# Weighing unit 1 of a mixture of softmaxes in pairs of heads

**Chip, cores, metric.** One core of one Trainium2 chip; the time is the device time of one launch in microseconds (us).

## The reference, cut to what matters

```python
batch, seq, vocab, num_heads = 32, 128, 4096, 4
prior_probs = softmax(prior)              # over the 4 heads
p = softmax(logits)                       # over the vocabulary, per head
mixture = sum over heads of prior_probs[..., None] * p
```

The 4096 rows (batch x seq) are worked in 32 units of 128 rows, counted from 0. A unit reads 4 heads x 128 rows x 16 KB = 8.39 MB and writes 2.10 MB, all float32.

## The kernel before

ScalarE takes the exponential of each head and sums it on the way; a reciprocal on VectorE and a small product on GpSimd make the four weights; VectorE adds up the four weighted heads ("terms", lines 175 and 181). `m` is how many heads are weighed at once: 4 in most units, 2 in the last four. The code is shortened; the waits for an output buffer to be stored are left out.

```python
es = (lt[:, 0], ebuf1, ebuf2, ebuf3)            # where head 0..3's exponentials go
def exp(h): ...      # ScalarE; for h > 0 it waits until unit u-1's term h has been read
def weigh(h, n): ... # n reciprocals on VectorE, n products on GpSimd; waits for exp h+n-1
def add(h): ...      # VectorE; add(0) overwrites the sum, add(1..3) add to it

m = H if u < U - 4 else 2
for h in range(H):
    if h == 2 and 0 < u < U - 3:
        store(u - 1, obuf[:, (u - 1) % 2], nc.scalar)   # issued by ScalarE, in its order
    exp(h, ...)
    if (h + 1) % m:
        continue
    g = h + 1 - m
    mul = weigh(g, m, ...)
    for k in range(g, h + 1):
        add(k, mul)
if u + 2 < U:
    load(u + 2)     # into the tile that unit u has read; waits for unit u's first term
```

There are two input tiles and two output buffers. All loads go through SyncE's queue, 28 of the 32 stores through ScalarE's.

The softmax here doesn't subtract the row's maximum and nothing guards it: scores larger than these inputs give would overflow.

Of the kernel before, what the change touches and what calls it, by code (L numbers as in the profile page):

```python
# [36 lines left out]
def kernel(  # L37
# [8 lines left out]
    B, S, H, V = logits.shape  # L46
# [6 lines left out]
    U = G * J  # L53
# [13 lines left out]
    def only(ins, *keep):  # L67
        for k in keep:
            tc.add_manual_dep(
                ins.ins,  # L70
                k.ins.name,
                mybir.DependencyInfo(mybir.DependencyClass.Sync, mybir.DependencyReason.DATA),
                reason="all that this instruction waits for",
            )
        tc.declare_no_dep(
            ins.ins,
            group="loop",
            keep=[k.ins for k in keep] + before.get(ins.ins.engine, []),
            reason="covered by the waits that are kept",
        )  # L80
        tc.add_to_no_dep_group("loop", ins.ins)
        before[ins.ins.engine] = [ins.ins]
        return ins
# [4 lines left out]
    exps = {}  # L88
    adds = {}
    stores = {}  # L90

    def load(u):
        if u == 0 or u >= U - 3:
            cuts = (0, 2, 3, 4) if u == U - 1 else (0, 2, 4)
        else:
            cuts = (0, H)
        for h, to in zip(cuts, cuts[1:]):
            ld = nc.sync.dma_start(  # L98
                out=ltile[:, u % 2, h:to], in_=lg[u // J, u % J, :, h:to, :]
            )  # L100


            if u >= 2:
                only(ld, adds[u - 2, 0] if h == 0 else exps[u - 2, to - 1])
            else:
                only(ld)
            for k in range(h, to):
                loads[u, k] = ld

    def store(u, acc, eng, lo=0, hi=V):  # L110
        st = eng.dma_start(out=ov[u // J, u % J, :, lo:hi], in_=acc[:, lo:hi])  # L111
        stores[u] = only(st, adds[u, H - 1])
# [18 lines left out]

    with tc.manual_schedule():
        load(0)
        nc.scalar.dma_start(out=pr, in_=pv)
        load(1)
        nc.gpsimd.memset(pn, 0.0)  # L136
        nc.vector.reduce_max(pmax, pr, axis=AX.X)  # L137
        nc.vector.tensor_sub(pr, pr, pmax.unsqueeze(2).to_broadcast([G, R, H]))  # L138
        nc.scalar.activation(pr, pr, AF.Exp)  # L139
        nc.vector.reduce_sum(pmax, pr, axis=AX.X)  # L140
        nc.vector.reciprocal(pmax, pmax)  # L141
        nc.vector.tensor_mul(  # L142
            pn[0:G].rearrange("g h r -> g r h"), pr, pmax.unsqueeze(2).to_broadcast([G, R, H])
        )
        pq = pn.rearrange("g h (p j) -> g j h p", j=J)
        for t in range(P // 32):
            nc.vector.transpose(pp[32 * t : 32 * (t + 1)], pq[:, :, :, 32 * t : 32 * (t + 1)])  # L147

        for u in range(U):
            bufd = u < U - 2  # L150
            lt = ltile[:, u % 2]
            acc = obuf[:, u % 2] if bufd else lt[:, 0]
            es = (lt[:, 0], ebuf1, ebuf2, ebuf3) if bufd else [lt[:, h] for h in range(H)]
            ppu = pp[:, u % J, :, u // J]

            def exp(h, *keep):
                ex = nc.scalar.activation(  # L157
                    es[h], lt[:, h], AF.Exp, accum_out=dsum[:, u, h : h + 1]
                )
                keep = (loads[u, h],) + keep  # L160
                if bufd and h and u:
                    keep += (adds[u - 1, h],)
                exps[u, h] = only(ex, *keep)

            def weigh(h, n, *keep):
                rc = nc.vector.reciprocal(rden[:, u, h : h + n], dsum[:, u, h : h + n])  # L166
                only(rc, exps[u, h + n - 1])
                mul = nc.gpsimd.tensor_mul(  # L168
                    coeff[:, u, h : h + n], rden[:, u, h : h + n], ppu[:, h : h + n]
                )  # L170
                return only(mul, rc, *keep)

            def add(h, mul, lo=0, hi=V):
                if h == 0:
                    st = nc.vector.tensor_scalar(  # L175
                        out=acc[:, lo:hi], in0=es[h][:, lo:hi], scalar1=coeff[:, u, h : h + 1],
                        scalar2=None, op0=ALU.mult,
                    )
                    adds[u, h] = only(st, mul)
                else:  # L180
                    st = nc.vector.scalar_tensor_tensor(  # L181
                        out=acc[:, lo:hi], in0=es[h][:, lo:hi], scalar=coeff[:, u, h : h + 1],
                        in1=acc[:, lo:hi], op0=ALU.mult, op1=ALU.add,
                    )
                    adds[u, h] = only(st, mul, adds[u, h - 1])



            free = (stores[u - 2],) if bufd and u >= 2 else ()

            m = H if u < U - 4 else 2
            for h in range(H):
                if h == 2 and 0 < u < U - 3:
                    store(u - 1, obuf[:, (u - 1) % 2], nc.scalar)
                exp(h, *(free if m == H and h == H - 1 else ()))
# [3 lines that stand above are left out]
                mul = weigh(g, m, *(free if m < H and g == 0 else ()))  # L199
                for k in range(g, h + 1):  # L200
                    n = 2 if u == U - 1 and k == H - 1 else 1
                    w = V // n
                    for c in range(n):
                        add(k, mul, c * w, (c + 1) * w)
                        if n > 1:
                            store(u, acc, nc.sync, c * w, (c + 1) * w)
            if u + 2 < U:
                load(u + 2)
            if u == U - 3:
                store(u - 1, obuf[:, (u - 1) % 2], nc.sync)  # L210
                store(u, acc, nc.sync)
            elif u == U - 2:
                store(u, acc, nc.sync)
# [30 lines left out]
```

## Time and profile before

| | before |
|---|---|
| median of 3 runs | 780.93 us (780.85 to 780.97) |
| busy: VectorE, ScalarE, GpSimd | 67%, 60%, 1% of the span |
| bytes moved | 335.65 MB, 431 GB/s over the span |
| one unit in the steady part | 24.17 us |

No compute engine is near its limit, and the bytes alone take most of the time. The prediction below shows the lines and reads them. In all lines of a profile DVE is VectorE, ACT is ScalarE, POOL is GpSimd and SP is SyncE; a q behind the name means the engine's sequencer, which issues transfers.

### The profile page before, as it was taken

What the parts mean: (1) busy time and instruction counts of PE and PEld (TensorE: products, weight loads), DVE (VectorE), ACT (ScalarE), POOL (GpSimd) and SP (SyncE); (2) the same over time, 40 slices, a digit from 0 to 9 for tenths busy, and PEclk for the clock granted to TensorE, in tenths of its full rate; (3) what the DMA queues carried; (4) which work ended last, traced back from release to release, by engine and by line L of the source; (5) the groups of instructions that cost most, each with busy time, mean ns of one, the idle gap of its engine ahead of it and who ended that gap; (6) DMA issues with size and microseconds to landing.
All of it is one profiled execution on the core that took longest, in us unless ns stands there. A gap on an engine that the chain in (4) does not pass through costs nothing.

```text
span 779.3 us, 628 instructions
## 1 busy us (share of the span) xinstructions
DVE 521.0 (67%) x174; ACT 470.0 (60%) x258; POOL 8.3 (1%) x41
## 2 busy tenths in 40 slices
DVE  4447865568655686556875558755587555788986
ACT  4476555765557655577555675556755567557782
POOL 0000000000000000000000000000000000000000
DMA  9999999999999999999999999999999999999998
GB/s 407 457 417 397 474 407 417 444 455 434 404 468 401 460 420 416 458 443 418 417 468 407 454 407 468 420 415 447 415 459 417 459 402 464 410 427 431 434 429 379
DMA packets 10117, 335.65 MB, mean 431 GB/s; under 512 B 1137, under 2 KB 1137, under 8 KB 1153
## 3 DMA queue, kind: packets, MB, share of 16 engines
q1 hardware_dynamic: 6048, 276.83, 82.3%
q10 hardware_dynamic: 4064, 58.79, 17.6%
q14 instruction: 5, 0.03, 0.0%
HBM read 268.50 MB, written 67.11 MB: 431 GB/s over the span
## 4 chain that ended last, share of the span: by engine, by line
DVE 55%; ACT 26%; DMA 15%; issue 2%; ACTq 1%; POOL 1%; DVEq 0%; SPq 0%; POOLq 0%
DVE obuf L181 45%; ACT ebuf L157 24%; DMA ltile<-in_logits_dram 9%; DVE obuf L175 8%; DMA out_dram<-obuf 6%; ACT ltile L157 1%; ACTq L111 1%; DVE ltile L181 1%; POOL coeff L168 1%; DVE rden L166 1%; DVEq L239 0%; SPq L98 0%; POOLq L239 0%; POOLq L168 0%
## 5 line engine op out<-in xcount | busy, mean ns | idle before, releaser
L181 DVE SCALAR_TENSOR_TENSOR obuf<-ebuf,coeff,obuf 128x4096 f32<-128x4096 f32 x90 | 403.6, 4484 | 3.8 <-POOL coeff L168 0.6
L157 ACT ACTIVATE ebuf<-ltile 128x4096 f32<-128x4096 f32 x90 | 323.7, 3597 | 39.6 <-DVE obuf L181 32.2
L157 ACT ACTIVATE ltile<-ltile 128x4096 f32<-128x4096 f32 x38 | 137.3, 3614 | 247.6 <-DMA ltile<-in_logits_dram 247.6
L166 DVE RECIPROCAL rden<-dsum 128x4 f32<-128x4 f32 (+1 forms) x36 | 6.3, 175 | 230.3 <-ACT ebuf L157 227.5
L175 DVE TENSOR_SCALAR obuf<-ltile,coeff 128x4096 f32<-128x4096 f32 x30 | 70.6, 2353 | 10.3 <-POOL coeff L168 10.3
L181 DVE SCALAR_TENSOR_TENSOR ltile<-ltile,coeff 128x4096 f32<-128x4096 f32 (+1 forms) x7 | 27.0, 3874 | 0.8 <-POOL coeff L168 0.6
L157 ACT ACTIVATION_READ_ACCUMULATOR ebuf<-ltile 128x1 f32 x90 | 16.8, 186 | 0.0
L168 POOL TENSOR_TENSOR coeff<-rden,pp 128x4 f32<-128x4 f32 (+1 forms) x36 | 7.2, 200 | 755.3 <-DVE rden L166 745.2
L157 ACT ACTIVATION_READ_ACCUMULATOR ltile<-ltile 128x1 f32 x38 | 7.1, 186 | 0.0
L175 DVE TENSOR_SCALAR ltile<-ltile,coeff 128x4096 f32<-128x4096 f32 x2 | 4.7, 2353 | 0.6 <-POOL coeff L168 0.6
L137 DVE TENSOR_REDUCE pmax<-pr 16x256 f32<-16x1024 f32 x1 | 1.2, 1206 | 5.4 <-DMA pr<-in_prior_dram 5.4
L139 ACT ACTIVATE pr<-pr 16x1024 f32<-16x1024 f32 x1 | 1.1, 1055 | 5.7 <-DVE pr L138 5.7
L142 DVE TENSOR_TENSOR pn<-pr,pmax 16x1024 f32<-16x1024 f32 x1 | 1.9, 1925 | 0.1
L140 DVE TENSOR_REDUCE pmax<-pr 16x256 f32<-16x1024 f32 x1 | 1.2, 1208 | 1.1 <-ACT pr L139 1.1
L139 ACT ACT_TABLE_LOAD x1 | 1.3, 1283 | 0.9 <-PEq L228 0.9
L147 DVE STREAM_TRANSPOSE pp<-pn 32x256 f32<-32x256 f32 x4 | 1.7, 436 | 0.1
L141 DVE RECIPROCAL pmax<-pmax 16x256 f32<-16x256 f32 x1 | 1.7, 1741 | 0.0
L138 DVE TENSOR_TENSOR pr<-pr,pmax 16x1024 f32<-16x1024 f32 x1 | 1.2, 1211 | 0.0
L136 POOL MEMSET pn<- 32x1024 f32 x1 | 0.9, 941 | 0.5 <-POOLq L228 0.5
L228 POOL MEMSET const-bfloat16-1.0<- 128x1 bf16 x1 | 0.1, 107 | 0.0
L228 POOL MEMSET const-uint8-127<- 128x1 uint8 x1 | 0.1, 107 | 0.0
L228 POOL MEMSET const-float32-0.0<- 128x1 f32 x1 | 0.1, 103 | 0.2 <-issue 0.2
(1 smaller groups left out, 0.1 us busy)
## 6 DMA issues: line engine op xcount, KB each, us to landing
out_dram<-obuf ACTq DMA_DIRECT2D x28, 2048.0 KB, 28.1
ltile<-in_logits_dram SPq DMA_DIRECT2D x7, 4096.0 KB, 25.5
ltile<-in_logits_dram SPq DMA_DIRECT2D x2, 2048.0 KB, 30.9
out_dram<-obuf SPq DMA_DIRECT2D x2, 2048.0 KB, 33.9
out_dram<-ltile SPq DMA_DIRECT2D x1, 2048.0 KB, 17.2
out_dram<-ltile SPq DMA_DIRECT2D x2, 1024.0 KB, 4.8
ltile<-in_logits_dram SPq DMA_DIRECT2D x28, 29.6
pr<-in_prior_dram ACTq DMA_DIRECT2D x1, 64.0 KB, 5.2
```

Source lines behind the costliest of these rows:

```text
L111: st = eng.dma_start(out=ov[u // J, u % J, :, lo:hi], in_=acc[:, lo:hi])
L137: nc.vector.reduce_max(pmax, pr, axis=AX.X)
L138: nc.vector.tensor_sub(pr, pr, pmax.unsqueeze(2).to_broadcast([G, R, H]))
L139: nc.scalar.activation(pr, pr, AF.Exp)
L141: nc.vector.reciprocal(pmax, pmax)
L142: nc.vector.tensor_mul(pn[0:G].rearrange("g h r -> g r h"), pr, pmax.unsqueeze(2).to_broadcast([G, R, H]))
L147: nc.vector.transpose(pp[32 * t : 32 * (t + 1)], pq[:, :, :, 32 * t : 32 * (t + 1)])
L157: ex = nc.scalar.activation(es[h], lt[:, h], AF.Exp, accum_out=dsum[:, u, h : h + 1])
L166: rc = nc.vector.reciprocal(rden[:, u, h : h + n], dsum[:, u, h : h + n])
L168: mul = nc.gpsimd.tensor_mul(coeff[:, u, h : h + n], rden[:, u, h : h + n], ppu[:, h : h + n])
L175: st = nc.vector.tensor_scalar(out=acc[:, lo:hi], in0=es[h][:, lo:hi], scalar1=coeff[:, u, h : h + 1], scalar2=None, op0=ALU.mult,)
L181: st = nc.vector.scalar_tensor_tensor(out=acc[:, lo:hi], in0=es[h][:, lo:hi], scalar=coeff[:, u, h : h + 1], in1=acc[:, lo:hi], op0=ALU.mu ...
```

## The change

Unit 1's sum should start after two exponentials and not after four. Its first term then ends before exponential 3 has read the tile, so load 3 must now name that exponential as well.

```diff
-                only(ld, adds[u - 2, 0] if h == 0 else exps[u - 2, to - 1])
+                free = [adds[u - 2, 0]] if h == 0 else []
+                if h or u == 3:
+                    free.append(exps[u - 2, to - 1])
+                only(ld, *free)
...
-            m = H if u < U - 4 else 2
+            m = 2 if u == 1 or u >= U - 4 else H
```

## The prediction

> **What bounds the kernel now.** I read the page first (busy shares, the DMA rows, the queues), then the stretches of the span, then the start of the timeline around units 0 to 2, then the queue's own waits and the end of the chain of waits. From the page:
>
> ```profile
> span 779.3 us, 628 instructions
> DVE 521.0 (67%) x174; ACT 470.0 (60%) x258; POOL 8.3 (1%) x41
> DMA  9999999999999999999999999999999999999998
> q1 hardware_dynamic: 6048, 276.83, 82.3%
> q10 hardware_dynamic: 4064, 58.79, 17.6%
> HBM read 268.50 MB, written 67.11 MB: 431 GB/s over the span
> ```
>
> No compute engine is busy more than 67% of the span. The DMA row is at its top digit in all 40 slices but the last, and the two queues add up to 82.3 + 17.6 = 99.9% of what 16 engines can be busy in the span. So the DMA engines have practically no idle time to give back. The stretches of the span (busy time by engine, then clock, DMA share, GB/s) say the same without the averaging:
>
> ```profile
> 1.30:41.70 40.40, 20.59 (x14) 16.59 (x10) 0.77 (x2) 1.00 1.00 431
> 112.50:693.50 581.00, 384.07 (x121) 351.05 (x193) 4.82 (x24) 1.00 1.00 433
> 693.50:749.30 55.80, 49.19 (x19) 43.74 (x25) 1.17 (x6) 1.00 1.00 432
> ```
>
> The reader is to see the last two columns: share 1.00 in the ramp, in the steady part and in the run-up to the end, always at 431 to 433 GB/s, although the compute engines' load differs a good deal. Each unit moves (268.50 + 67.11) / 32 = 10.49 MB, and 10.49 MB at 433 GB/s is 24.2 us. All 335.6 MB at 433 GB/s are 775 us; start-up before the first bytes and the last wait make the rest of the span.
>
> Now the place that the change touches. Unit 0's first exponential starts at 12.67 us, unit 1's at 41.73, unit 2's at 64.72. From the timeline (start, duration, engine and operation, and in brackets the idle time before it and what ended it):
>
> ```profile
> 41.73 3.62 ACT L157 ACTIVATE ltile<-ltile 128x4096 f32<-128x4096 f32 x1 [12.04 <-DMA ltile<-in_logits_dram]
> 45.35 3.60 ACT L157 ACTIVATE ebuf<-ltile 128x4096 f32<-128x4096 f32 x1
> 56.05 0.18 ACT L157 ACTIVATION_READ_ACCUMULATOR ebuf<-ltile 128x1 f32 x1
> 56.27 0.18 DVE L166 RECIPROCAL rden<-dsum 128x4 f32<-128x4 f32 x1 [10.13 <-ACT ebuf L157]
> 56.76 2.35 DVE L175 TENSOR_SCALAR obuf<-ltile,coeff 128x4096 f32<-128x4096 f32 x1 [0.32 <-POOL coeff L168]
> 59.15 13.52 DVE L181 SCALAR_TENSOR_TENSOR obuf<-ebuf,coeff,obuf 128x4096 f32<-128x4096 f32 x3
> 64.72 3.62 ACT L157 ACTIVATE ltile<-ltile 128x4096 f32<-128x4096 f32 x1 [8.48 <-DMA ltile<-in_logits_dram]
> 71.84 0.19 ACT L157 ACTIVATION_READ_ACCUMULATOR ebuf<-ltile 128x1 f32 x1
> 72.70 0.34 ACTq L111 DMA_DIRECT2D out_dram<-obuf  x1
> 73.09 3.59 ACT L157 ACTIVATE ebuf<-ltile 128x4096 f32<-128x4096 f32 x1 [1.06 <-DVE obuf L181]
> 88.32 3.62 ACT L157 ACTIVATE ltile<-ltile 128x4096 f32<-128x4096 f32 x1 [7.92 <-DMA ltile<-in_logits_dram]
> ```
>
> VectorE idles 10.13 us before unit 1's reciprocal: that is the wait that the change attacks. But ScalarE waits for a load before every unit (12.04, 8.48, 7.92 us), and those are the waits that the bytes set.
>
> **What the Trainium skill says.** "DMA: Bandwidth & Descriptors", section "Where 436 GB/s comes from", puts the ceiling of a core's 16 engines at 435.2 GB/s; this trace holds 433 over 581 us, so it agrees and nothing is left above. The same page, "Issuing engines are not separate DMA queues", says that transfers started by different engines run on the same 16 DMA engines and interleave. The trace fits: the stores issued by ScalarE take their 17.6% out of the same 99.9%, and a 2 MB store needs a median 28.1 us to land. So a transfer that is started earlier takes its share from another one in flight. "Perfetto Trace Analysis", section "Optimization Strategy", says to look for gaps on the engine that is the bottleneck and to make what blocks it start sooner. Here that is the DMA, and it has no gap where the change acts.
>
> **The change part by part.**
>
> Removed: unit 1's first term no longer needs exponentials 2 and 3. Exponential 1 with its read-out ends at about 49.04 (45.35 + 3.60, and 0.09 by the read-out). Before, the last read-out ended at 56.23 and the first term began at 56.76, 0.53 later; the same 0.53 gives 49.57 now. VectorE is free by then (unit 0's last term ends at 46.14). First term 49.57 to 51.94, second term (4.49 + 0.03) to 56.46.
>
> Added: one reciprocal (0.18) and one GpSimd product (0.20). The second pair's reciprocal sits behind the second term in VectorE's order; by 56.46 all exponentials are done (56.23), so it costs the same hop less the first wait, about 0.49: third term from 56.95, fourth from 61.47, done at 65.96. Before it was done at 72.67. Unit 1's sum is thus ready 6.7 us sooner, after paying 0.5 us of new hops inside what was idle time.
>
> Moved: two transfers.
> - Load 3 overwrites unit 1's tile. Before it followed the first term (59.13). Now it must follow the first term (51.94) and, by the added condition, exponential 3 (56.23), so it is issued near 56.3: 2.9 us earlier. It stands in the same queue behind load 2, which lands at 64.7 in either case. The 5.6 us that load 3 waits behind it become 8.4 us. Worth on the path: 0.
> - Store 1 is issued by ScalarE in order, after unit 2's second exponential, which ends at 72.03 because load 2 landed at 64.7. So of the 6.7 us only 72.70 - 72.05 = 0.65 us survive. Unit 2's third exponential follows: 72.4 in place of 73.09.
>
> From there on the chain of waits shows a closed loop: two exponentials 7.32, reciprocal and product 0.5, terms 2.36 + 3 x 4.50, store issue 0.34, gaps; 24.17 us from 72.70 to 96.86 and in nearly every unit after. It would carry the 0.65 us forward as earlier stores. The loads, though, follow the bytes. In the steady part ScalarE reaches unit u's third exponential 1.1 to 1.9 us before VectorE lets it go on; this slack shrinks by up to 0.65 us and stays positive or becomes a wait for a load. The sum on the end: removed bytes 0, added DMA gaps 0, so 0 us.
>
> **The end of the kernel.** This decides whether earlier stores can be cashed in:
>
> ```profile
> 701.57 18.07 DMA out_dram<-obuf
> 722.38 26.87 DMA ltile<-in_logits_dram
> 749.28 7.32 ACT ltile L157 x4
> 764.35 4.50 DVE ltile L181
> 768.87 2.35 DVE ltile L181
> ```
>
> The final stretch hangs on a load that lands at 749.28. Before that load the engines have moved all earlier loads and all 28 ScalarE stores (the last one landed about 719.7), and they never paused. So its landing is the sum of those bytes over the rate, whatever the order within. From 749.28 to the last half store (4.8 us to land) nothing of unit 1 takes part. If stores become 0.65 us earlier, load 29 may land that much later, and loads 30 and 31 land when they did.
>
> **The rivals.**
>
> (a) The compute loop is the true bound. For it: its period is the same 24.17 us as the DMA's to the second decimal, and the chain of waits follows it from 72.7 to 701.6 with hardly a gap. Then the 0.65 us reach the end: 780.3. Against it: 8 us of load wait in each unit, and engines without idle time. I give this part of a chance, since two equal periods cannot be told apart in one trace.
>
> (b) The earlier load 3 and store 1 collide. A 2 MB store is 4.8 us of all engines at 433 GB/s; started 0.65 us sooner it takes at most about that from load 3, which lands at up to 88.9 in place of 88.3. Unit 3's slack before its third exponential was 1.6 us, so it is absorbed; if it were not, 781.5.
>
> (c) Head or tail noise: an instruction more on VectorE and GpSimd, another phase of the two queues when the last loads come. The three runs of before span 0.12 us; I allow some tenths, 780.6 to 781.3.
>
> (d) The gain goes through whole: 6.7 us less, 774.2. It would need idle DMA time of that length, which is not there.
>
> **Range and chances.** The central step gives 780.93 + 0 = 780.9. Rival (a) pulls to 780.3, (b) to 781.5, so 8 in 10 lie in 780.3 to 781.4. A change of 2% is 15.6 us, more than twice the whole 6.7 us set free, and slower by 2% would need a DMA gap that nothing here opens: 0.005, 0.99, 0.005.
>
> **What would show it.** Right: unit 1's first term at about 49.6, its last one ending near 66.0; load 3 issued near 56.3, but unit 2 still starting at 64.7 and unit 3 at 88.3 to 88.9; store 1 at about 72.05; DMA share 1.00 at 431 to 433 GB/s as before; the last load landing at 749.3 within a few tenths. It is wrong if unit 2 or 3 starts over 1 us earlier, if the landing at 749.3 moves by over 0.5 us, or if a stretch shows a DMA share well below 1.

## The result, and the profile after

| | runs | median | range |
|---|---|---|---|
| before | 6 | 780.93 us | 780.84 to 781.11 |
| after | 6 | 781.20 us | 781.16 to 781.49 |

The ratio is 1.0004, with a 95% interval of 0.9991 to 1.0017: the same time. (A ratio is the mean time of one kernel's fast runs over that of the other's fast runs of the same rounds, so not quite the ratio of the medians.) The 0.27 us between the medians lie within that interval.

The span is the same (779.3 us in both profiles), yet the chain of waits is a different one. From the page of the kernel before, and below it from that of the changed kernel (shares of the span by engine):

```profile
DVE 55%; ACT 26%; DMA 15%; issue 2%; ACTq 1%; POOL 1%; DVEq 0%; SPq 0%; POOLq 0%
```

```profile
DMA 64%; ACT 27%; DVE 6%; issue 1%; POOL 0%; DVEq 0%; POOLq 0%; ACTq 0%
```

VectorE's terms were 55% of what the end hung on and are 6% now; loads have taken their place. The waits say it in microseconds. Of the kernel before, then of the changed one (who waited for whom, total us, times, longest):

```profile
ACT ltile L157 <- DMA ltile<-in_logits_dram: 247.6, 32, 12.0
...
ACT ebuf L157 <- DVE obuf L181: 32.2, 26, 1.9
```

```profile
ACT ltile L160 <- DMA ltile<-in_logits_dram: 282.2, 32, 12.1
```

ScalarE's 32.2 us of waiting for VectorE are gone (no such line is left), and its waiting for loads has grown by 34.6 us. The change removed a wait in 26 units by touching one, and longer waits for loads took its place.

Here is where it happens. From the timeline of the changed kernel (start, duration, engine and operation; idle time before it):

```profile
49.64 2.35 DVE L178 TENSOR_SCALAR obuf<-ltile,coeff 128x4096 f32<-128x4096 f32 x1 [0.31 <-POOL coeff L171]
...
56.90 9.01 DVE L184 SCALAR_TENSOR_TENSOR obuf<-ebuf,coeff,obuf 128x4096 f32<-128x4096 f32 x2 [0.31 <-POOL coeff L171]
64.31 3.62 ACT L160 ACTIVATE ltile<-ltile 128x4096 f32<-128x4096 f32 x1 [7.98 <-DMA ltile<-in_logits_dram]
65.93 0.34 ACTq L114 DMA_DIRECT2D out_dram<-obuf  x1
...
71.52 3.56 ACT L160 ACTIVATE ebuf<-ltile 128x4096 f32<-128x4096 f32 x1
...
88.50 3.62 ACT L160 ACTIVATE ltile<-ltile 128x4096 f32<-128x4096 f32 x1 [9.69 <-DMA ltile<-in_logits_dram]
...
95.29 0.34 ACTq L114 DMA_DIRECT2D out_dram<-obuf  x1
```

Unit 1's first term starts at 49.64 (before: 56.76) and its last one ends at 65.91. Store 1 goes out at 65.93, 6.77 us sooner than before. Unit 2's third exponential follows its second at 71.52 without a gap (before: 73.09). Store 2 is 1.57 us sooner (95.29 against 96.86). But unit 3 starts at 88.50 against 88.32: its load came no sooner. So the gain is 6.77 us at store 1, 1.57 at store 2 and 0 at load 3. The later stores keep a part of it (ScalarE's last one goes out at 700.71 against 701.57), but the loads do not: the last one lands at 749.09 against 749.28.

### The profile page after: what moved, and what is told of

Same layout as the page of the kernel before. It is cut to its first block, busy times and chain, and to the rows that moved or that the text cites. A ratio compares the mean times of both kernels' runs of the same rounds, so it can differ in the third digit from the quotient of the medians.

```text
span 779.3 us, 631 instructions
## 1 busy us (share of the span) xinstructions
DVE 521.1 (67%) x175; ACT 467.7 (60%) x258; POOL 8.5 (1%) x42
## 3 DMA queue, kind: packets, MB, share of 16 engines
q1 hardware_dynamic: 6048, 276.83, 82.2%
## 4 chain that ended last, share of the span: by engine, by line
DMA 64%; ACT 27%; DVE 6%; issue 1%; POOL 0%; DVEq 0%; POOLq 0%; ACTq 0%
DMA ltile<-in_logits_dram 62%; ACT ebuf L160 19%; ACT ltile L160 7%; DVE obuf L178 5%; DMA out_dram<-obuf 2%; DVE ltile L184 1%; POOL coeff L171 0%; DVE rden L169 0%; DVEq L243 0%; POOLq L243 0%; ACTq L114 0%; POOLq L171 0%
```

## The experiments

Two theories were set against each other. **B**: the bytes alone set the time. **L**: the closed loop (two exponentials, weights, four terms, the store's issue, and the next unit's third exponential behind it) is a bound of its own, with nearly the same period as the DMA. With both at 24.17 us the trace of before cannot tell which leads. So the first experiments cut the bytes, the next stretch the loop, and the last move load 3 alone.

### Half of the store bytes

```diff
     def store(u, acc, eng, lo=0, hi=V):
+        if eng is nc.scalar:
+            hi = V // 2
         st = eng.dma_start(...)
```

The edit was made to the kernel before, to the changed one, and to one in which every unit is weighed in pairs (`m = 2` throughout, and every load waits for the last exponential too). Their outputs are wrong, which doesn't matter for the times.

> The kernel before, but ScalarE's 28 stores write only half of each row (wrong on purpose): 29.4 MB less of 335.6, so 306.2 MB. Theory B (the bytes alone set the time): 306.2 MB at 433 GB/s are 707 us, plus 4 us at both ends, 711 to 715 us. Theory L (the closed loop of exponentials, terms and store issue, 24.17 us a unit, is a bound of its own right behind the bytes): the middle keeps 24.17 us a unit from unit 2 to 28 while the loads arrive ahead of it, and only the tail shrinks; 745 to 770 us, with the DMA share well below 1.

> The changed kernel with the same half stores. Theory B: the same 711 to 715 us as the kernel before with half stores, within 0.5 us. Theory L: now the loop is what binds, so what unit 1 saves reaches the end; it is limited by unit 2's second exponential, so 1.5 to 3.5 us less than the kernel before with half stores.

> Half stores, and every unit weighed in pairs. This opens the loop: the first two terms no longer wait for the last two exponentials, and the bound of the compute side falls to VectorE's 16 to 17 us a unit. Theory B: 711 to 715 us as without pairs. Theory L: far faster than both other half-store kernels, at the bytes' 711 to 725 us, since now the loop is gone and the DMA binds again.

Measured, against 780.96 us (780.88 to 781.12) of the kernel before in the same rounds:

| half stores | median | range | ratio to before |
|---|---|---|---|
| kernel before | 775.92 us | 775.87 to 776.02 | 0.9936 |
| changed kernel | 773.13 us | 772.97 to 773.27 | 0.9900 |
| all units in pairs | 713.89 us | 713.79 to 714.06 | 0.9141 |

Theory B fails for the first two: 29.4 MB less of traffic, some 68 us at 433 GB/s, brought 5 us. Theory L holds in kind, though its time and its DMA share for the first kernel were missed (see below). With the loop opened in every unit the time falls to 713.9, in the range that the bytes gave; so the narrower stores are not slow in themselves. And between the first two kernels the change is worth 775.92 - 773.13 = 2.79 us: in this setting the loop binds, and a head start for the loop reaches the end (store 2 goes out at 93.91 against 96.73, 2.82 us sooner). From the stretch of the span between 125 and 650 us (the last two columns are DMA share and GB/s), for the kernel before with half stores, then for all pairs with half stores:

```profile
125.00:650.00 525.00, 348.89 (x110) 319.70 (x174) 4.42 (x22) 1.00 0.98 390
```

```profile
125.00:650.00 525.00, 386.32 (x145) 353.02 (x195) 9.45 (x48) 1.00 1.00 434
```

The first line is the surprise. The DMA moves 390 GB/s where it can move 434, and its busy share still reads 0.98. A busy share near 1 is thus no proof that the DMA is full; the rate beside it has to be read. The chain of waits of the kernel before with half stores shows the loop itself, one piece to a line (start, us, what):

```profile
97.11 7.32 ACT ebuf L159 x4
...
104.71 0.21 POOL coeff L170
...
104.94 2.36 DVE obuf L177
...
107.33 4.50 DVE obuf L183
...
120.89 0.34 ACTq L113
```

It recurs with a period of 24.16 us (store issues at 72.56, 96.73, 120.89), the same as with full stores, although a unit now needs only 9.44 MB / 434 GB/s = 21.8 us of the DMA. My 745 to 770 us for the first kernel were too low: I expected a shorter tail, but ScalarE's last store is issued at 701.10 us (701.57 with full stores), because the loop paces everything up to there, and what follows shrank by only some 5 us.

### Every unit in pairs, full stores

> Full stores, right result, every unit weighed in pairs. Bytes unchanged. If the bytes bind with full stores, as the prediction says: 780.5 to 781.6 us, no gain, with all ScalarE waits turned into waits for loads. If the compute loop is what holds the kernel at 24.17 us a unit and the DMA could go faster: below 775 us.

Correct, 781.62 us (781.57 to 781.93), ratio to before 1.0009 (0.9994 to 1.0024). Opening the loop in every unit brings nothing when the bytes are whole. Loads now pace all units, with starts 24.17 us apart (211.24, 235.40, ... 404.59 us for units 8 to 16), and ScalarE waits for no term any more, only for loads:

```profile
ACT ltile L160 <- DMA ltile<-in_logits_dram: 285.5, 32, 12.0
```

So the DMA's period is 24.17 and the loop's 24.16 us: two bounds that lie within about 0.01 us of each other. Fewer bytes alone brought 5 us, opening the loop alone nothing. The 0.7 us above the kernel before are just more than I expected. From 56 to 125 us this kernel moved 423 GB/s against 433, and its last load landed at 749.72 against 749.28 us; why the DMA was slower there I did not find.

### A longer loop

```diff
                 rc = nc.vector.reciprocal(rden[:, u, h : h + n], dsum[:, u, h : h + n])
                 only(rc, exps[u, h + n - 1])
+                for _ in range(4 if h == 0 else 0):
+                    rc = nc.vector.reciprocal(rden[:, u, h : h + n], dsum[:, u, h : h + n])
+                    only(rc, exps[u, h + n - 1])
```

> The kernel before with unit's first reciprocal done five times over (four more of 0.18 us with their issue, some 0.7 us a unit, in the stretch between the exponentials and the first term). Theory B: ScalarE waits 8 us for a load in each unit, so 0.7 us are absorbed: 781 us. Theory L: the loop has the same period as the DMA, so it becomes 24.9 us and binds; 26 units x 0.7 less the slack of 1.1 is +17 us: 793 to 800 us.

> The changed kernel with the same extra reciprocals. Theory B: 781 us. Theory L: the head start of 1.5 us that the change gives the loop is used up after two or three units, then the loop binds at 24.9 us a unit: 1 to 2 us below the slowed kernel before, 792 to 799 us.

> Every unit in pairs, with the same extra reciprocals. Both theories: VectorE needs some 17.5 us of 24.2 and no loop through the store issue is left, so 780.5 to 782 us. If this one is slow as well, the extra reciprocals cost something else than the loop.

Measured, all correct, against 781.03 us of the kernel before in the same rounds:

| with the extra reciprocals | median | range | ratio to before |
|---|---|---|---|
| kernel before | 802.89 us | 802.15 to 806.83 | 1.0290 |
| changed kernel | 800.75 us | 800.44 to 801.35 | 1.0255 |
| all units in pairs | 782.53 us | 782.38 to 782.82 | 1.0020 |

Theory B again fails for the first two: 8 us of waiting for a load in each unit did not absorb anything. I had the right sign and the wrong size, as the chain of waits of the first of them shows:

```profile
106.37 0.19 DVE rden L169
106.56 0.02 issue
106.58 0.19 DVE rden L169
...
123.45 0.34 ACTq L111
```

Each reciprocal costs 0.19 + 0.02 us, so four cost 0.84 and not 0.7; the store issues are 25.01 us apart (98.44, 123.45). 26 units x 0.84 are 21.8 us; measured 21.9. The 1.1 us that I took off as slack were not the loop's: in the kernel before it is ScalarE that waits for VectorE for that long, so the loop had none. The change takes 2.1 us off (1 to 2 expected), as store 2 goes out 2.25 us sooner (96.19 against 98.44) and later stores keep that distance. Here too the DMA's share misleads. From 125 to 650 us of the kernel before with the longer loop:

```profile
125.00:650.00 525.00, 350.59 (x189) 306.38 (x169) 4.21 (x21) 1.00 1.00 420
```

Share 1.00 at 420 GB/s. With pairs everywhere the extra work costs 0.9 us in place of 21.9 (0.5 us more than I had allowed).

### Load 3 alone

Both edits start from the changed kernel and hold load 3 back, with everything else as it is:

```diff
                 if h or u == 3:
                     free.append(exps[u - 2, to - 1])
+                if u == 3:
+                    free.append(adds[1, 2])      # third term; in the second kernel adds[1, 3]
```

> The changed kernel, but load 3 is held back until unit 1's third term is done (61.5 us in place of 56.4), later even than in the kernel before (59.1). Load 2 lands at 64.3, so the queue still has work when load 3 joins it. Theory B: no change against the changed kernel, within 0.3 us: when load 3 is issued counts for nothing as long as the DMA has other work. A theory in which the earlier issue of load 3 is what the change is worth: 2 to 5 us more.

> The same, but load 3 waits for unit 1's fourth term (66.0 us), after load 2 has landed at 64.3. Then the load queue runs dry for about 2 us and the time from issue to first bytes; what is left of store 0 and the start of store 1 fill part of it. Theory B: the idle DMA time shows in the end one for one: 1 to 3.5 us more than the changed kernel, with a DMA share below 1 only in the stretch from 62 to 70 us. Theory L: the loop would absorb it within 2 units (ScalarE waits 8 us for loads anyway): under 0.5 us.

The first took 781.05 us (780.89 to 781.09; before 781.03 in the same rounds; ratio 1.0000, 0.9987 to 1.0013). So with load 3 issued even later than in the kernel before, the changed kernel takes the same time: the earlier issue is worth nothing at the end, as long as load 2 is still under way when load 3 joins the queue. It is worth something on the way: unit 3 now starts at 89.68 and not at 88.50, store 3 goes out at 120.66 against 119.48 (before: 121.03), and so most of the head start is lost. ScalarE's wait for VectorE is back:

```profile
ACT ebuf L162 <- DVE obuf L186: 29.4, 24, 2.0
```

Whichever of the two ends last, the time is the same, as two bounds of one period would have it. The second, 4.5 us later still, took 783.94 us (783.69 to 784.21; ratio 1.0037, 1.0024 to 1.0051). Windows of the changed kernel, then of this one:

```profile
56.00:100.00 44.00, 25.54 (x9) 26.34 (x17) 0.40 (x2) 1.00 1.00 433
100.00:125.00 25.00, 15.98 (x5) 15.35 (x9) 0.20 (x1) 1.00 1.02 443
```

```profile
56.00:100.00 44.00, 25.49 (x9) 22.04 (x15) 0.40 (x2) 1.00 1.00 420
100.00:125.00 25.00, 15.98 (x5) 15.45 (x10) 0.20 (x1) 1.00 0.97 414
```

(433 - 420) x 44 us + (443 - 414) x 25 us = 1.30 MB were not moved by 125 us, and 1.30 MB at 433 GB/s are 3.0 us. The time rose by 2.7 us against the changed kernel's median (of other rounds) and by 2.9 against the kernel before, which by the same windows was 2.4 us of bytes ahead. The dip lies where I expected it: from 62 to 70 us the share is 0.80 at 295 GB/s, against 0.91 at 393 in the changed kernel. What I wrote for theory L, under 0.5 us, failed: the loop starts late itself (store 3 at 123.72) and goes on at 24.17 us a unit. The DMA rate that is lost here is not won back by the end. That neither the DMA nor the loop can run faster than 24.17 us a unit would explain it; no run tests this by itself.

No experiment points to a version that beats both kernels: with the loop opened in every unit the core still moves the same bytes at 433 to 434 GB/s.

## Why the prediction was right, point by point

- **The time.** 780.9 said, 781.2 measured, in the range of 780.3 to 781.4. The central argument holds: the bytes are unchanged and moved at 433 GB/s throughout, and the end hangs on a load whose landing is the sum of all bytes before it. That load landed at 749.09 us (749.28 before; said: within some tenths).
- **What the DMA share was taken to prove.** This step was weak. "Share 1.00" and "99.9% of what 16 engines can be busy" were read as no idle time to give back. The half-store and longer-loop runs show shares of 0.98 and 1.00 at 390 and 420 GB/s. What carried the conclusion was the other column, 433 GB/s. The Trainium skill says so ("Perfetto Trace Analysis", section "Identifying the Most-Contended Engine": for DMA occupancy misleads, as there are 16 engines, and HBM utilization is to be used instead), and the runs agree: the rate tells them apart, the share does not.
- **Unit 1.** First term at 49.57 said, 49.64 found; the last one done at 65.96 said, 65.91 found; load 3 issued at 56.3 said, 56.4 found.
- **Store 1.** This step failed: "Store 1 is issued by ScalarE in order, after unit 2's second exponential", at 72.05. It went out at 65.93, in the middle of unit 2's *first* exponential (64.31 to 67.93). The trace of before had shown it: store 0 at 46.17 lies inside an exponential that ran from 45.35 to 48.95. The Trainium skill has the mechanism ("Perfetto Trace Analysis", section "DVE / Act Engine Instruction"): the sequencer pushes an engine instruction into a wait queue and goes on. So the head start of the loop was 1.57 us at store 2 and not 0.65, and ScalarE's wait for VectorE vanished in all units. I had allowed for that ("becomes a wait for a load"), so the sum did not suffer.
- **Loads 2 and 3.** Unit 3 starts at 88.50, within the 88.3 to 88.9 given to rival (b), which costs nothing. Unit 2 starts at 64.31, 0.41 us sooner than said. The earlier load 3 is not the reason: with load 3 held back unit 2 starts at 64.27 and 64.26. The cause stays open.
- **Rival (a).** "The compute loop is the true bound" got "part of a chance", since "two equal periods cannot be told apart in one trace". The runs tell them apart: the loop is a true bound of 24.16 us, and the DMA is another of 24.17. What the prediction lacked is that both can bind at once. The DMA's bound is why the range held: had the head start of 1.57 us reached the end, as it would by rival (a), the time would have been about 779.4. The evidence it used against the loop, 8 us of load wait in each unit, was no evidence: the longer loop cost 21.9 us with those waits in place.

## What to carry to other kernels

A wait was removed here and the end did not move, because something else had the same period. Cut the bytes and stretch or open the loop in throwaway kernels, and you see each bound by itself. Read DMA saturation from GB/s, not from the busy share alone. When an issue is moved earlier, ask whether its queue would have run dry without it: here 5 us of delay cost nothing while load 2 was under way, and 4.5 us more, with the queue dry, cost 2.9 us that stayed to the end.

## What the Trainium skill lacked or had wrong

- "Perfetto Trace Analysis", section "DMA Engine Tracks", says that a DMA engine's slices show actual busy time without idle time. In these runs the share that the profile makes from DMA records stays at 0.98 with 390 GB/s and at 1.00 with 420 GB/s, while 434 GB/s also gives 1.00. The records of the same 276.83 MB in SyncE's queue (all loads and the last stores) fill 82.3% of 779.3 us (641 us) in the kernel before and 88.7% of 774.1 us (687 us) with half stores: they get longer when there is less to do, so their length seems to hold more than the moving of bytes.
- "DMA: Bandwidth & Descriptors", section "Where 436 GB/s comes from", says that for transfers between HBM and SBUF the HBM side at about 358 GB/s binds. In this program of one core, 8 MB loads beside 2 MB stores ran at 433 GB/s over 581 us, near the 435.2 GB/s that the same section gives for the fabric of 16 SBUF ports (the prediction took that figure for the core's 16 engines). The same section calls a measured 425 GB/s near fabric-rate, so the sentence is too general as it stands; other pages of the skill give the figure of 358 with a condition.
- No page found says in so many words that loads and stores of one core add up to one limit. Here they do: 268.5 MB read and 67.1 MB written moved at 433 GB/s, and 268.5 MB with 37.8 MB (half stores, in pairs) at 434.
